# Layer 0's first mixer projections from unsplit fp32 weights, and V's last four blocks kept back

## The chip, the core and the metric

The kernel runs on one core of a Trainium2 chip. The time is device microseconds of one execution. The engines are named as in the profile: PE is TensorE (PEld its weight loads), DVE VectorE, ACT ScalarE, POOL GpSimd, SP SyncE, whose queue issues every DMA of this kernel. The times given are three runs of the kernel and one more execution that the hardware profiler recorded.

## What is computed

Two layers on x (256 tokens by 1024, fp32). A layer modulates a normalised x by vectors that come from a conditioning vector c, projects it into chunks, mixes tokens in three ways (a state-space mixer with a convolution, block-sparse attention, sliding-window attention), adds the result, and then looks up product-key experts.

```python
cond = jax.nn.silu(c)
for l in range(DEPTH):
    mod = cond @ ada_w[l] + ada_b[l]
    sh1, sc1, g1, sh2, sc2, g2 = [m[:, None, :] for m in jnp.split(mod, 6, axis=-1)]
    h = rms_norm(x, norm1_g[l]) * (1.0 + sc1) + sh1
    proj = h @ w_in[l]
    z, xbc, dt_raw, mq, mk, mv, sq, sk, sv = jnp.split(proj, offsets, axis=-1)
    ...
    y = jnp.concatenate([y_ssd, y_moba, y_swa], axis=-1) @ w_out[l]
    x = x + g1 * y
    h = rms_norm(x, norm2_g[l]) * (1.0 + sc2) + sh2
    x = x + g2 * peer_ffn(h, peer_wq[l], peer_k1[l], peer_k2[l], peer_u[l], peer_v[l])
return rms_norm(x, final_g)
```

`peer_ffn` makes queries h @ wq for 8 heads, scores them against two key sets, keeps the top 16, and sums act times V over 16384 experts; here that is computed densely, U first (128 blocks of 128 experts), then V.

## The kernel before, in words

**Split products.** Nearly every product is made from reduced-precision parts: `split` (L151) turns a fetched weight tile into a high part (ScalarE cast, L159, tile `wH`) and a low part (a subtraction, L162, tile `wL`; on VectorE for "v", on GpSimd in two halves for "h"), and `mm3` (L165) does three matmuls, high x high, high x low, low x high. h is split in the same way into `hs` (`hH`, `hL`; L258, L259). Weight tiles come through `fetch` (L145), a ring of five `raw` tiles of 512 KB; `wH` and `wL` are rings of three.

**Layer 0's start.** `cond_row` (L117) loads c as one row, spreads it over 128 partitions with two matmuls against ones (L127) and applies SiLU. A modulation column is one VectorE operation (`ada_use`, L177): a row tile of `ada` (512.5 KB) times the row of c, summed. Layer 0 needs 40 such rows (vectors 0 to 4, eight each); they come through the same `raw` ring as the weights. The first 16 give the shift and scale of h; h is made in four quarters of 256 channels (`norm_banks` L237 transposes x into PSUM, `norm_h` L245 scales it). While the quarters come, the chunks mq, mk and sq are projected in pieces that the table `FIRST` orders (L46). The other 24 rows are handed out two per fetched tile by `later` (L455). After the scores of the MoBA heads the stages run in the order of the string `ORDER` (L47): `rest` is the chunk with the values and dt, c0 to c3 convolve the chunks xbc0 to xbc3, mv, mp, ss, sv, sp are MoBA values and output and the same of the sliding window (with its own chunk sk), seg, tok, stb, cb and st belong to the state-space mixer, z0 and z1 are gates.

**The scheduler.** The program is written in this order, and a scheduler with a model of its own then puts each engine's instructions into a fixed list; each engine runs its list in order.

**Experts.** In `peer` (L671) the queries go head by head (`query`, L713), the split of their weights half on GpSimd. U and V stages follow with TensorE in a steady stream; `steps` (L952) gives, in layer 0's V stage, another c row and 56 modulation rows for layer 1, through `ada_ahead` (L184), which fetches three rows ahead into four tiles. V sums 128 blocks into four PSUM banks (`v_parts`, L888); the last two (`LAST = 2`, L56) are taken bank by bank, so that the first banks are finished earlier. Then the residual is added, the next layer's norm is taken, or at the end the final norm and the output.

```python
            first = {n: [bank(b) for b in kinds] for n, kinds in (("mq", ("pa", "pa")), ("mk", ("pa", "pa")), ("sq", ("pb", "pb")))}
            part = {n: proj_parts(pcs, wl, *off[n], 2) for n, pcs in first.items()}
            for p, names in enumerate(FIRST):
                banks = norm_banks(xn, p, 1, "pc")
                ...
                norm_h(xp, banks, colt, modc, COLS["n1"], 0, 1, p)
                for n in post.split():
                    next(part[n])
```

Of the kernel before, what the change touches and what calls it, by code (L numbers as in the profile page):

```python
# [45 lines left out]
FIRST = (("- - - mq", "mq"), ("mk mk - sq sq", "mq mk sq"), ("mq - mk -", "mq mk"), ("sq sq", "mq mk sq"))  # L46
ORDER = "rest c0 mv c1 mp seg ss c2 z0 sv c3 tok stb z1 cb st sp"  # L47
# [8 lines left out]
LAST = 2  # L56
# [25 lines left out]
def trunk(ctx: ExitStack, tc: tile.TileContext, x_in, c_in, ada, cols, rows, w_in, w_out, wq, keysT, uT, vT, fg, out, dbg=None):  # L82
# [67 lines left out]

    def split(src, low="v", pool=None):  # L151
# [4 lines left out]
        else:  # L156
            h = pool.tile([P, 1024], F32R, tag="oH", name="oH", bufs=2)
            lo = pool.tile([P, 1024], F32R, tag="oL", name="oL", bufs=2)
# [21 lines left out]
    def ada_steps(l, m, modc, pool):  # L180

        return [lambda k=k: ada_use(m, k, fetch(ada[l, m * KD + k]), modc, conds[pool]) for k in range(KD)]

    def ada_ahead(jobs, pool):  # L184

        items = [(l, m, k, modc) for l, m, modc in jobs for k in range(KD)]
# [3 lines left out]
        def load(i):  # L190
            if i < len(items):
                l, m, k = items[i][:3]
                held[i] = pool.tile([P, D + 1], F32, tag="adaw", name="adaw", bufs=AHEAD + 1)
                nc.sync.dma_start(held[i], ada[l, m * KD + k])

        def step(i):
# [5 lines left out]
            ada_use(m, k, held.pop(i), modc, conds[pool])  # L202
# [10 lines left out]
    def norm_rows(pool, xt, c):  # L213

        ss = pool.tile([P, 2], F32, tag="hs", name="hs", bufs=2)
        for n in range(2):
            junk = pool.tile([P, 512], F32, tag="t2k", name="junk", bufs=3)
            A.activation(junk, xt[:, c, n * 512:(n + 1) * 512], AF.Square, scale=1.0 / 32.0, accum_out=ss[:, n:n + 1])  # L218
# [5 lines left out]

    pin = [None]
# [19 lines left out]
    def norm_h(pool, banks, colt, modc, gcol, sh, sc, k20=0):  # L245
# [684 lines left out]
    for l in range(DEPTH):  # L930
        ada0 = {}

        def early(pool, k0, n):
            if l:
                return []
# [118 lines left out]
```

## Time and profile before

| what | value |
|---|---|
| three runs | 1953.8, 1957.2, 1955.97 us; median 1955.97 |
| the profiled execution | 1956.04 us, its span 1954.3 us |
| granted TensorE clock, mean | 0.981 |
| busy: PE, DVE, ACT, POOL | 1875.9, 1430.5, 966.3, 498.1 us |
| share of the span: PE, DVE, ACT, POOL | 96%, 73%, 49%, 25% |
| DMA moved | 376.53 MB, 193 GB/s over the span |
| modulation rows through `raw`, through `adaw` | 40 and 56 issues of 512.5 KB |

The shares are means over stages that differ: most of the span is the U and V stages, where PE is always busy. How the 78 us in which PE is not busy lie in time is read from stretches of the span, and what ends a wait there from the waits and the timeline. A row of the timeline begins with its start and its duration; matmuls overlap, so the cost of one is the distance to the next one's start.

### The profile page before, as it was taken

To read this page: it belongs to the slowest core of one execution; us is meant where nothing else is said; L and a number is where in the kernel's file an instruction comes from. 1 tells how busy PE (TensorE), PEld (TensorE's weight loads), DVE (VectorE), ACT (ScalarE), POOL (GpSimd) and SP (SyncE) were. 2 spreads that over 40 slices of the span, in tenths; PEclk is the share of its full clock that TensorE was granted. 3 is DMA by queue.
4 is the path that set the end of the run, shared out by engine and by line. 5 is a ranking of instruction groups with operands and counts; after the bars stand their busy time and mean duration, and the time that the engine had idled before them with its cause. 6 is when DMAs were issued, how large, how long until landed. Compare 5 with 4: busy or idle time off the path is not lost. (4 is left out here: it accounts for less than half of the span.)

```text
span 1954.3 us, 33671 instructions
## 1 busy us (share of the span) xinstructions
PE 1875.9 (96%) x12864; PEld 1714.5 (88%) x12864; DVE 1430.5 (73%) x2679; ACT 966.3 (49%) x1502; POOL 498.1 (25%) x303
## 2 busy tenths in 40 slices
PE   4898999999999999999989989999999999999998
PEld 3786999999999888888878789999999998888886
DVE  6866799889963898966667669968899346666665
ACT  3464445444444454545547444455444445555544
POOL 5675799100024001000001167960000320000001
PEclk8898999999999999999989989999999999999999
DMA  7863455444455999866543344554444555655553
GB/s 276 288 211 116 162 182 182 167 162 153 161 166 172 380 348 350 312 199 195 192 131 123 118 143 150 186 178 159 160 155 160 173 193 190 223 196 193 193 194 116
DMA packets 103557, 376.53 MB, mean 193 GB/s; under 512 B 12002, under 2 KB 12258, under 8 KB 102756
## 3 DMA queue, kind: packets, MB, share of 16 engines
q1 hardware_dynamic: 103396, 374.39, 56.3%
q8 instruction: 100, 1.64, 0.3%
q14 instruction: 61, 0.50, 0.1%
HBM read 371.20 MB, written 3.15 MB: 192 GB/s over the span
## 5 line engine op out<-in xcount | busy, mean ns | idle before, releaser
L159 ACT CAST wH<-raw 128x1024 fp32r<-128x1024 f32 (+1 forms) x602 | 629.3, 1046 | 530.7 <-PE pu L167 349.9
L162 DVE TENSOR_TENSOR wL<-raw,wH 128x1024 fp32r<-128x1024 f32 x437 | 535.3, 1226 | 223.6 <-ACT wH L159 222.8
L162 POOL TENSOR_TENSOR wL<-raw,wH 128x512 fp32r<-128x512 f32 (+2 forms) x224 | 438.4, 1977 | 595.7 <-ACT wH L159 586.0
L166 PE MATMUL pu<-hH,wH 128*128 128x256 f32 x2048 | 581.2, 284 | 3.9 <-ACT act L693 3.9
L168 PE MATMUL pu<-hH,wL 128*128 128x256 f32 x2048 | 575.7, 281 | 0.0
L167 PE MATMUL pu<-hL,wH 128*128 128x256 f32 x2048 | 575.4, 281 | 0.0
L167 PE MATMUL pacc<-wL,aH 128*128 128x512 f32 x1024 | 399.2, 390 | 0.0
L168 PE MATMUL pacc<-wH,aL 128*128 128x512 f32 x1024 | 398.5, 389 | 0.0
L166 PEld LDWEIGHTS pu<-hH,wH 128*128 128x128 f32 x2048 | 386.9, 189 | 4.6 <-ACT act L693 4.6
L167 PEld LDWEIGHTS pu<-hL,wH 128*128 128x128 f32 x2048 | 387.1, 189 | 0.0
L168 PEld LDWEIGHTS pu<-hH,wL 128*128 128x128 f32 x2048 | 386.5, 189 | 0.0
L166 PE MATMUL pacc<-wH,aH 128*128 128x512 f32 x1024 | 277.4, 389 | 0.0
L892 ACT CAST aH<-act 128x256 fp32r<-128x256 f32 x256 | 104.0, 408 | 340.3 <-PE pacc L167 339.0
L167 PEld LDWEIGHTS pacc<-wL,aH 128*128 128x128 f32 x1024 | 192.2, 188 | 40.4 <-DVE wL L162 0.8
L168 PEld LDWEIGHTS pacc<-wH,aL 128*128 128x128 f32 x1024 | 192.2, 188 | 39.7
L166 PEld LDWEIGHTS pacc<-wH,aH 128*128 128x128 f32 x1024 | 192.1, 188 | 39.8
L893 DVE TENSOR_TENSOR aL<-act,aH 128x256 fp32r<-128x256 f32 x256 | 108.4, 425 | 108.6 <-ACT aH L892 108.2
L980 POOL TENSOR_TENSOR x<-x,fgb 128x512 f32<-128x512 f32 x2 | 3.4, 1700 | 352.4 <-ACT junk L218 352.4
L166 PE MATMUL pa<-hH,wH 128*128 128x256 f32 x256 | 75.7, 308 | 12.5 <-ACT hH L258 8.7
L167 PE MATMUL pa<-hL,wH 128*128 128x256 f32 x256 | 76.4, 301 | 1.9 <-DVE hL L259 1.8
L168 PE MATMUL pa<-hH,wL 128*128 128x256 f32 x256 | 75.6, 299 | 0.9 <-POOL wL L162 0.9
L854 DVE SCALAR_TENSOR_TENSOR act<-pc,act 128x160 f32<-128x160 f32 (+30 forms) x126 | 38.5, 306 | 44.5 <-PE pc L848 44.3
(428 smaller groups left out, 2470.9 us busy)
## 6 DMA issues: line engine op xcount, KB each, us to landing
raw<-in_uT_dram SPq DMA_DIRECT2D x256, 512.0 KB, 3.6
raw<-in_vT_dram SPq DMA_DIRECT2D x256, 512.0 KB, 4.4
adaw<-in_ada_dram SPq DMA_DIRECT2D x56, 512.5 KB, 5.9
raw<-in_ada_dram SPq DMA_DIRECT2D x40, 512.5 KB, 4.9
raw<-in_w_in_dram SPq DMA_DIRECT2D x38, 512.0 KB, 4.8
raw<-in_wq_dram SPq DMA_DIRECT2D x32, 512.0 KB, 3.6
raw<-in_w_out_dram SPq DMA_DIRECT2D x16, 512.0 KB, 3.9
raw<-in_w_in_dram SPq DMA_DIRECT2D x8, 392.0 KB, 3.5
```

The source lines that it names most:

```text
L159: A.copy(h[:, :n], src)
L162: eng.tensor_tensor(out=lo[:, o:o + step], in0=src[:, o:o + step], in1=h[:, o:o + step].bitcast(F32), op=ALU.subtract)
L166: T.matmul(o, l[0], r[0], start=start, stop=False)
L167: T.matmul(o, l[0], r[1], start=False, stop=False)
L168: T.matmul(o, l[1], r[0], start=False, stop=stop)
L854: V.scalar_tensor_tensor(out=a, in0=pv[:, lo:hi, :], scalar=1.0 / WSCALE, in1=a, op0=ALU.mult, op1=ALU.mult)
L892: A.copy(aH, act)
L893: V.tensor_tensor(out=aL, in0=act, in1=aH.bitcast(F32), op=ALU.subtract)
L980: (V if c else G).tensor_tensor(out=xt[:, c, cs], in0=xt[:, c, cs], in1=fgb[:, cs], op=ALU.mult)
```

## The change

Six edits. (1) In layer 0 the chunks mq, mk, sq, xbc0 and xbc1 are projected together, from unsplit fp32 weights and unsplit h; two column blocks share a PSUM bank, which five matmuls with a zero tile clear first. The weights come through `fetch_whole`, every second one into a `wH` or `wL` tile. h is kept in four tiles of `wt`, its split parts `hs` are made after the MoBA scores are issued. `rest` and sk use the unsplit products too; in `ORDER` the two convolutions c0 and c1 come before mv. (2) Layer 0's 40 rows go through `ada_ahead` with four tiles (`oH`, `oL`) of their own. (3) c is loaded into all 128 partitions by one broadcast DMA and SiLU is applied in place; x is loaded in two halves, and the second half's squares are summed by VectorE. (4) In layer 1 mq is unsplit, and the parts of h are split behind its products. (5) In both layers query 0 is unsplit and the parts of h are made after it; query 1's low half is made by VectorE. (6) Of V's last blocks four are taken bank by bank instead of two; two of them get their own tiles `held`, in the place of the row pool, which is closed 14 blocks before the end; a layer's residual and norm are written row half by row half.

```diff
+WHOLE0 = "mq mk sq xbc0 xbc1"
+FIRST = (
+    ((WHOLE0, WHOLE0), ("", WHOLE0), (WHOLE0, WHOLE0), ("", WHOLE0)),
+    (("- - - mq", "mq"), ("mk mk - sq sq", "mq mk sq"), ("mq - mk -", "mq mk"), ("sq sq", "mq mk sq")),
+)
+ORDER = (
+    "rest c0 c1 mv ss mp seg c2 z0 sv c3 tok stb z1 cb st sp",
+    "rest c0 mv c1 mp seg ss c2 z0 sv c3 tok stb z1 cb st sp",
+)
...
-LAST = 2
+LAST = 4
+HELD = 2
+ADA_END = 14
...
-        nc.sync.dma_start(row[0:1, 0:D], c_in)
-        ones = st.tile([1, P], F32, tag="raw", name="ones", bufs=RB)
-        G.memset(ones, 1.0)
-        pcs = []
-        for n in range(2):
-            pc = small_bank()
-            T.matmul(pc, ones, row[0:1, n * 512:(n + 1) * 512], start=True, stop=True)
-            pcs.append(pc)
-        for n, pc in enumerate(pcs):
-            A.activation(row[:, n * 512:(n + 1) * 512], pc, AF.Silu)
+        nc.sync.dma_start(row[:, 0:D], c_in.to_broadcast([P, D]))
+        A.activation(row[:, 0:D], row[:, 0:D], AF.Silu)
...
+    def fetch_whole(src):
+
+        n = src.shape[-1]
+        spare[0] += 1
+        if spare[0] % 2:
+            return fetch(src)
+        tag = "wH" if spare[0] % 4 else "wL"
+        t = st.tile([P, 1024], F32, tag=tag, name="whole", bufs=HB)
+        nc.sync.dma_start(t[:, :n], src)
+        return t[:, :n]
...
+    def proj_parts_whole(pcs, src, off, w, step, hw, zeroed=False):
...
+                        T.matmul(pc[:, :S], raw[:, kk * w + cb * P:kk * w + (cb + 1) * P], hw[k // 2][:, k % 2, :], start=k == 0 and not zeroed, stop=k == KD - 1 and (not zeroed or cb == len(pcs) - 1))
...
+                zero = new([P, 4, P], "segr")
+                V.memset(zero, 0.0)
+                for n in WHOLE0.split():
+                    pc = bank("pb" if n == "sq" else "pa")
+                    T.matmul(pc, zero[:, 0, :], zero, start=True, stop=False)
+                    first[n] = [pc[:, b * S:(b + 1) * S] for b in range(2)]
+                    part[n] = proj_parts_whole(first[n], wl, *off[n], 2, whole, True)
...
             def query(h):
-                with pinned() if h == 0 else nullcontext():
-                    pq = proj_channels(wq[l], h * D * 256, 256, lambda q: "h")
+                if h == 0:
+
+                    pq = [bank() for _ in range(2)]
+                    for _ in proj_parts_whole(pq, wq[l], 0, 256, 4, whole2):
+                        pass
+                    for f in whole2_halves:
+                        f()
+                else:
+                    with pinned() if h == 1 else nullcontext():
+                        pq = proj_channels(wq[l], h * D * 256, 256, lambda q: "v" if h == 1 else "h")
...
-            spread(pend, min(1.0, (n + 1) / (NKEY - 8)), len(todo))
-        last = [v_parts(n, low(n)) for n in range(NKEY - LAST, NKEY)]
+            spread(pend, min(1.0, (n + 1) / (NKEY - ADA_END)), len(todo))
+            if n == NKEY - ADA_END:
+
+                right.close()
+                held = right.enter_context(tc.tile_pool(name=f"held{l}", bufs=1, reuse_waits="tile", side="right"))
+        last = [v_parts(n, low(n), held if n < NKEY - LAST + HELD else None) for n in range(NKEY - LAST, NKEY)]
...
+    own = lambda i: mx.tile([P, D + 1], F32, tag="oL" if i % 2 else "oH", name="adaw", bufs=2)
+    adas = ada_ahead([(0, (0, 1), mod[0])] + [(0, (m,), mod[0]) for m in (2, 3, 4)], own, conds[mx]) if l == 0 else []
```

SyncE's queue at the start of layer 0, first before (behind the loads of the columns, c, x and `rowt`; `in_ada` are the modulation rows, `in_w_in` weight halves):

```order
L148 DMA raw<-in_ada_dram 128x1025 x4
L174 DMA colt<-in_cols_dram 128x112
L148 DMA raw<-in_w_in_dram 128x1024
L148 DMA raw<-in_ada_dram 128x1025
L148 DMA raw<-in_w_in_dram 128x1024
L148 DMA raw<-in_ada_dram 128x1025 x3
```

and now, from the same place (`whole` is a weight half in a `wH` or `wL` tile):

```order
L204 DMA adaw<-in_ada_dram 128x1025 x4
L149 DMA raw<-in_w_in_dram 128x1024
L162 DMA whole<-in_w_in_dram 128x1024
L149 DMA raw<-in_w_in_dram 128x1024
L162 DMA whole<-in_w_in_dram 128x1024
L149 DMA raw<-in_w_in_dram 128x1024
L188 DMA colt<-in_cols_dram 128x112
L204 DMA adaw<-in_ada_dram 128x1025 x8
```

Five weight halves now follow the first four rows at once, and rows and weights no longer share one ring.

VectorE's list around the third xbc chunk, before: `ynam` are the normalised MoBA rows, `conv` with 128x255 the first step of a convolution.

```order
L178 SCALAR_TENSOR_TENSOR raw,modc<-raw,crow 128x1025
L376 TENSOR_SCALAR ynam<-conv,yamr 128x256
L207 TENSOR_SCALAR yamm<-ss 128x1
L178 SCALAR_TENSOR_TENSOR raw,modc<-raw,crow 128x1025
L475 SCALAR_TENSOR_TENSOR conv<-pa,colt,conv 128x255
L475 SCALAR_TENSOR_TENSOR conv<-pa,colt,conv 128x254
L376 TENSOR_SCALAR ynam<-conv,yamr 128x256
```

Now, at the same rows of the MoBA norm:

```order
L443 TENSOR_SCALAR ynam<-conv,yamr 128x256
L217 TENSOR_SCALAR yamm<-ss 128x1
L192 SCALAR_TENSOR_TENSOR adaw,modc<-adaw,crow 128x1025
L443 TENSOR_SCALAR ynam<-conv,yamr 128x256
L192 SCALAR_TENSOR_TENSOR adaw,modc<-adaw,crow 128x1025 x2
L423 SCALAR_TENSOR_TENSOR yL<-pc,colt,yH 128x256
L423 SCALAR_TENSOR_TENSOR yL<-pa,colt,yH 128x256
L192 SCALAR_TENSOR_TENSOR adaw,modc<-adaw,crow 128x1025 x2
```

The convolution of xbc1 has moved ahead of the MoBA norm; 36 of the 40 rows stand before its last `ynam`, where 34 did.

TensorE's list ahead of the third xbc chunk, now (`L420` transposes `ynam`, `L644` is seg, `L180` the first split product of xbc2):

```order
L636 MATMUL pb<-a,mgt 128x8
L637 MATMUL pb<-a,mle 128x8
L420 MATMUL pc<-ident,ynam 128x128
L420 MATMUL pa<-ident,ynam 128x128
L644 MATMUL pa<-segr,mgt 128x512
L420 MATMUL pc<-ident,ynam 128x128
L420 MATMUL pa<-ident,ynam 128x128
L644 MATMUL pc<-segr,mgt 128x512
L180 MATMUL pc<-hH,wH 128x256
```

Before, the same place read:

```order
L353 MATMUL pa<-ident,ynam 128x128
L353 MATMUL pb<-ident,ynam 128x128
L553 MATMUL pb<-segr,mgt 128x512
L406 MATMUL pc<-sk,sq 128x128
L407 MATMUL pc<-sk,sq 128x256
L406 MATMUL pb<-sk,sq 128x128
L407 MATMUL pb<-sk,sq 128x256
L553 MATMUL pa<-segr,mgt 128x512
```

The scores of the sliding window, which stood between the MoBA transposes and xbc2, have moved ahead of the transposes.

## Rows read from the trace of the kernel before

**Rows 1.** Busy time of each engine (instructions), granted clock, DMA share, GB/s, by stretch.

```profile
40.00:60.00 20.00, 13.35 (x86) 12.54 (x87) 17.21 (x26) 7.41 (x14) 11.06 (x7) 0.74 0.82 283
80.00:100.00 20.00, 16.22 (x114) 14.38 (x112) 19.27 (x35) 10.66 (x17) 17.41 (x11) 0.92 0.78 280
650.00:700.00 50.00, 50.00 (x230) 41.57 (x229) 48.62 (x75) 23.58 (x36) 0.00 (x0) 1.00 1.01 389
900.00:950.00 50.00, 50.00 (x223) 41.39 (x222) 30.78 (x37) 24.46 (x36) 0.00 (x0) 1.00 0.60 197
```

The columns are the stretch, its length, then PE, PEld, DVE, ACT, POOL, the clock as a share of full speed, the DMA engines' busy share and GB/s.

**Rows 2.** Waits of SyncE's queue, 0 to 200 us: total, times, longest.

```profile
SPq L148 <- POOL wL L162: 64.5, 28, 4.9
SPq L148 <- DVE raw L178: 49.7, 28, 5.9
```

**Rows 3.** Timeline, 22.5 to 24 us: two modulation rows on VectorE and a GpSimd split.

```profile
22.66 1.23 DVE L178 SCALAR_TENSOR_TENSOR raw<-raw,crow 128x1025 f32<-128x1025 f32 x1
...
23.04 1.98 POOL L162 TENSOR_TENSOR wL<-raw,wH 128x512 fp32r<-128x512 f32 x1 [3.01 <-ACT wH L159]
...
23.80 2.31 DVE L178 SCALAR_TENSOR_TENSOR raw<-raw,crow 128x1025 f32<-128x1025 f32 x1
```

**Rows 4.** Groups by line and shape, VectorE, 0 to 125 us: busy, mean ns, waits.

```profile
L178 DVE SCALAR_TENSOR_TENSOR raw<-raw,crow 128x1025 f32<-128x1025 f32 x40 | 61.1, 1538 | 11.2 <-DMA raw<-in_ada_dram 7.5 <-POOL wL L162 2.0 <-ACT crow L130 1.7
```

**Rows 5.** Timeline of TensorE: starts of matmuls that follow each other.

```profile
58.34 0.59 PE L407 MATMUL pa<-mk,mq 64*128 64x256 f32 x2
58.77 0.27 PE L406 MATMUL pa<-mk,mq 64*128 64x128 f32 x1
...
104.63 1.02 PE L553 MATMUL pb<-segr,mgt 128*128 128x512 f32 x2
105.58 0.49 PE L406 MATMUL pc<-sk,sq 64*128 64x128 f32 x2
...
200.48 0.28 PE L166 MATMUL pc<-hH,wH 128*128 128x256 f32 x1
200.60 0.28 PE L167 MATMUL pc<-hL,wH 128*128 128x256 f32 x1
```

**Rows 6.** Timeline, marks of layer 0: waited h, its last quarter, xbc2's first matmul, the masked product.

```profile
45.29 1.22 PE L166 MATMUL pa<-hH,wH 128*128 128x256 f32 x4 [6.75 <-ACT hH L258]
...
50.83 0.55 DVE L257 TENSOR_SCALAR h<-pc,acol,modc 128x256 f32<-128x256 f32 x1
...
110.46 0.39 PE L166 MATMUL pa<-hH,wH 128*128 128x256 f32 x1
...
145.90 0.69 DVE L587 TENSOR_TENSOR cbm<-pb,mle 128x512 f32<-128x512 f32 x1 [2.29 <-PE pb L585]
```

**Rows 7.** Timeline, layer 0's second norm to the first query's scores.

```profile
179.22 0.89 DVE L234 TENSOR_SCALAR xn<-x,hr 128x512 f32<-128x512 f32 x2 [0.44 <-POOL hr L222]
...
180.89 2.88 DVE L234 TENSOR_SCALAR xn<-x,hr 128x512 f32<-128x512 f32 x2 [0.66 <-POOL hr L222]
...
185.90 0.58 PE L166 MATMUL pa<-hH,wH 128*128 128x256 f32 x1 [0.96 <-ACT hH L258]
...
200.84 1.05 PE L725 MATMUL pa<-kt,q 128*128 128x128 f32 x8
```

**Rows 8.** Timeline of TensorE in layer 0's V stage: the conditioning row.

```profile
645.17 1.12 PE L127 MATMUL pb<-crow,ones 1*128 1x512 f32 x2
...
647.08 0.50 PE L167 MATMUL pacc<-wL,aH 128*128 128x512 f32 x1
```

**Rows 9.** The broadcast load of the last gain, from the view of that tile.

```profile
DMA to landing us min/median/max: 8.5/8.5/8.5
```

**Rows 10.** Timeline of TensorE between the layers.

```profile
990.53 0.39 PE L167 MATMUL pacc<-wL,aH 128*128 128x512 f32 x1
990.76 0.39 PE L168 MATMUL pacc<-wH,aL 128*128 128x512 f32 x1
...
1000.31 0.56 PE L166 MATMUL pa<-hH,wH 128*128 128x256 f32 x1
```

**Rows 11.** Timeline, the end: the last matmul and the last output operation of ScalarE.

```profile
1944.77 0.39 PE L168 MATMUL pacc<-wH,aL 128*128 128x512 f32 x1
...
1950.34 0.72 ACT L986 ACTIVATE o<-x,hr 128x512 f32<-128x512 f32 x1 [1.29 <-POOL hr L222]
```

More of the change, by code (lines that the diff above doesn't have):

```diff
@@ L256, in norm_h, with half @@
                 else:
-                    V.tensor_scalar(out=h32[:, q, :], in0=src, scalar1=acol[:, k:k + 1], scalar2=modc[:, sh, k:k + 1], op0=ALU.mult, op1=ALU.add)
-            A.copy(hs[0][:, 2 * k2:2 * k2 + 2, :], h32)
-            V.tensor_tensor(out=hs[1][:, 2 * k2:2 * k2 + 2, :], in0=h32, in1=hs[0][:, 2 * k2:2 * k2 + 2, :].bitcast(F32), op=ALU.subtract)
+                    d = V.tensor_scalar(out=h32[:, q, :], in0=src, scalar1=acol[:, k:k + 1], scalar2=modc[:, sh, k:k + 1], op0=ALU.mult, op1=ALU.add)
+                    done[0] = d.ins
+                    if whole is not None and len(banks) > 1:
+                        pin[0] = d.ins
+            def half(k2=k2, h32=h32):
+                A.copy(hs[0][:, 2 * k2:2 * k2 + 2, :], h32)
+                V.tensor_tensor(out=hs[1][:, 2 * k2:2 * k2 + 2, :], in0=h32, in1=hs[0][:, 2 * k2:2 * k2 + 2, :].bitcast(F32), op=ALU.subtract)
+            if whole is None:
+                half()
+            else:
+                halves.append(half)
+        return halves
     def gated_add(pool, xt, c, n, acc, gb):
@@ L450, in put @@
                     put_y(self.yn, self.blk0, 2)
-            todo = late(mx)
+            todo = list(late)
             due = [0.0]
@@ L463, in conv @@
             def conv(q):
-                for cb, pc in enumerate(proj_channels(wl, *off[f"xbc{q}"])):
+                for cb, pc in enumerate(first.get(f"xbc{q}") or proj_channels(wl, *off[f"xbc{q}"])):
                     b = 2 * q + cb
@@ L503, in mixers @@
             tick[0] = later
+            if l == 0:
+                proj_tokens_rest = lambda: proj_tokens_whole(wl, *off["rest"], whole)
+            else:
+                proj_tokens_rest = lambda: proj_tokens(wl, *off["rest"])
             mq = to_sb(first["mq"], "mq")
@@ L509, in mixers @@
             moba.scores()
+            if halves:
+                with tc.issue_after(done[0]):
+                    for f in halves:
+                        f()
             vx = new([P, NC, 6, 65], "vx")
@@ L518, in values_dt @@
             def values_dt():
-                for c, pc in enumerate(proj_tokens(wl, *off["rest"])):
+                for c, pc in enumerate(proj_tokens_rest()):
                     V.tensor_tensor(out=dtp[:, c, :], in0=pc[:, 0:8], in1=rowt[:, 0:8], op=ALU.add)
@@ L610, in mixers @@
             }
-            for name in ORDER.split():
+            for name in ORDER[l].split():
                 stages[name]()
@@ L976, in trunk @@
             rs.append(norm_rows(xp, xt, c))
+            if not last:
+                xn.append(norm_scaled(xp, xt, c, rs[c]))
         if last:
@@ L987, in trunk @@
                 nc.sync.dma_start(out[0, c * P:(c + 1) * P, cs], o)
-        else:
-            xn = [norm_scaled(xp, xt, c, rs[c]) for c in range(NC)]
         if dbg:
```

137 lines of the change are left out of this document (94 added, 43 removed).

## The prediction

> **What bounds the kernel now.** I read the busy shares by stretch first. In the middle of the program TensorE has no gap: 50.00 of 50 us between 650 and 700 us and again between 900 and 950, with VectorE and ScalarE at 48.62 and 23.58 and at 30.78 and 24.46 [rows 1]. What an edit saves off TensorE there is nothing, and what it takes from TensorE there counts in full. Layer 0's first mixer is another matter: between 40 and 60 us TensorE is busy for 13.35 of 20 us at a granted clock of 0.74, and VectorE for 17.21; between 80 and 100 VectorE has 19.27 of 20 and GpSimd 17.41, while the DMA engines move only 280 GB/s against 389 at 650 us [rows 1]. The waits of SyncE's queue say why they move so little: in the first 200 us it stood 64.5 us behind low halves that GpSimd was still making and 49.7 us behind modulation rows that VectorE was still using, because both sit in the ring of five `raw` tiles [rows 2]. And the two engines slow each other: the use of one modulation row took 1.23 us at 22.66 and 2.31 us at 23.80, under a split that GpSimd began at 23.04 [rows 3]; over the first 125 us the forty took 61.1 us, 1.538 each [rows 4]. So this stage is held by VectorE, GpSimd and buffers, not by TensorE.
>
> **The price of an unsplit product.** A split product is three matmuls 0.12 us apart, 0.36 us for 256 columns [rows 5]. An unsplit fp32 one is two instructions in the trace. The nearest rows bound it: a score matmul with 256 columns but 64 rows of weights took 0.43 us for its two halves (58.34 to 58.77), and one with 128 rows and 512 columns took 0.95 us (104.63 to 105.58), so 0.475 for half the columns [rows 5]. I take 0.43, between 0.40 (no drain) and 0.475. It costs TensorE 0.07 us more than the split one and frees ScalarE and GpSimd or VectorE of the split.
>
> A rule prices it too. The Trainium skill's page "FP8 and Floating Point Precision", section "TensorE Precision Notes", says that true fp32 goes through the array in four passes, where the split product here has three. By that alone it would be 4 x 0.12 = 0.48 us, an estimate; the rows with 64 and 128 weights stand on either side of it. With it the last burst of the first stage, 20 products, would end 20 x 0.05 = 1 us later, and the forecast would be 1943 instead of 1942.
>
> **Layer 0's first stage.** Before, the last quarter of h was made at 50.83 us and the MoBA scores began at 58 us (the row at 58.34) with mq, mk and sq done [rows 5, 6]. Now xbc0 and xbc1 are done beside them. The last quarter waits, on VectorE, for the 19th modulation row. Until that has landed the queue has to bring 19 x 0.525 MB, ten weight halves of 0.524, x with 1.05 and the broadcast c with 0.52: 16.8 MB from about 3 us on. At 283 GB/s that ends at 62 us, at 389 at 46 [rows 1]. I take 355 GB/s, so 50.5 us: nearer the upper end, since ten weight halves now have ten places (five `raw`, three `wH`, two `wL`) and the modulation rows four of their own, which removes the two waits of [rows 2]. With the last use (1.2 us) and the column scale the last quarter of h is there at about 51.5; its 20 products cost 20 x 0.43 = 8.6 us, and 1 us goes to a slow clock. The scores begin at 61 us, 3 us later than before, but with 32 products more behind them. The five zero matmuls (0.95 us each by the 512-column row, twice that at half clock) run while x is still on its way, so they cost nothing; without that cover they would cost 5 to 10 us.
>
> **From the scores to the third convolution chunk.** Before, xbc2's matmuls began at 110.46, 52.1 us after the scores [rows 5, 6]. They stand behind the transposes of the normalised MoBA rows, which VectorE makes late in its list. Now the list has no convolution matmuls to wait for, but the same VectorE work: 17 modulation rows, all scores, the dt chain, the convolutions of xbc0 and xbc1. Added: four splits of h that were moved here, 4 x 0.7 = 2.8 us. Saved: GpSimd splits only xbc2 and half of z0 in this time (6 half splits of some 2 us, where it was busy for 17.41 of 20 us before [rows 1]), so 17 x (1.538 - 1.23) = 5.2 us of contention on the rows, half as much again on the other operations, 8 in all; and 17/40 of the 9.5 us that VectorE waited for rows and for GpSimd [rows 4], 4 us. 52.1 + 2.8 - 8 - 4 = 43. TensorE's own work there (rest, MoBA values, sk and the scores, of which rest's 16 products of 392 columns and sk's 8 are 2.3 us dearer unsplit) is some 22 us and hides. So xbc2 begins at 61 + 43 = 104, **6 us earlier**. From there on to the masked C*B product at 145.90 [rows 6] the same four split chunks are left and TensorE is nearly full in both kernels; I take 0 for that, and 0 for what follows up to the residual.
>
> **First query, both layers.** Before, x's second half was scaled in 2.88 us, under six half splits by GpSimd, the first product of query 0 stood at 185.90, and scores at 200.84 [rows 7]. Now query 0 is not split and query 1 is split by VectorE, so the scaling should cost 0.89, as the other half did at 179.22 [rows 7], and the first product needs neither the cast nor the low half: some 2.7 us earlier. Against that 16 x 0.07 = 1.1 us at full clock. Net 1.7 in layer 0, 1.5 in layer 1, where the list is the same. The moved splits of h (four casts, four subtractions) lie under query 0's 7 to 9 us.
>
> **Between the layers.** The two `ones` matmuls of the conditioning row go: TensorE stands at them from 645.17 to 647.08 [rows 8], 1.9 us in a full stage. In their place a broadcast DMA; the like one for the last gain landed after 8.5 us [rows 9], so VectorE may wait some 3 us, which its slack and three split buffers hide. After V's last matmul at 990.76 the first product came at 1000.31 [rows 10]. With four blocks kept back, the sums of rows 0 to 127 are finished 24 matmuls before the end, 0.23 us apart [rows 10], so 5.4 us, instead of 12 matmuls, 2.7, and mq starts from h itself: I take 2.5 us off and 1.1 us on for mq unsplit, **1.4**. Keeping back four blocks costs no TensorE time: VectorE and ScalarE have 40% and 50% to spare there [rows 1] and two blocks get their own places.
>
> **The end.** The last matmul starts at 1944.77, the last output operation at 1950.34 [rows 11]. Rows 0 to 127 will be out of the way by then: 0.9 us.
>
> Sum: 6 + 1.7 + 1.5 + 1.9 + 1.4 + 0.9 = 13.4 us. The profiled execution took 1956.04 (its span 1954.3), the median 1955.97, so they are one: 1956.0 - 13.4 = 1942.6, **1942**.
>
> **Rivals.** (a) *TensorE and DMA set the pace, VectorE does not.* If contention was most of VectorE's load and the DMAs run at 389 GB/s, the scores come at 57 and xbc2 after TensorE's 22 us, say at 84: 26 us earlier instead of 6, 1922. For it: 2.31 against 1.23 us [rows 3]. Against it: in-order, VectorE has 36 of 40 rows ahead of the transposes.
> (b) *The DMA rate stays.* If 283 GB/s is what rows of this size get in a mixed queue, h's last quarter comes at 64, scores at 73.5, xbc2 at 117: 6 us later, which eats the other terms: 1955.
> (c) *TensorE becomes the bound, slower.* The first stage now has 80 products in four bursts with waits for h between; before, TensorE waited 6.75 us for h until 45.29 us [rows 6], and the stretch from 40 to 60 us had a granted clock of 0.74, between the levels of 1.2 and 2.4 GHz [rows 1]. If every burst runs at 1.2 GHz, the stage has 80 x 0.86 = 69 us from 17 us on, the scores come at 86 instead of 61, and the sum turns to 1942 + 25 = 1967. It decides from the point where the scores come 13.4 us later than forecast, at 74 us. Against the whole price speaks the 0.92 between 80 and 100 us, where TensorE was busy for 16.22 of 20 us and waited often [rows 1].
> The Trainium skill ("TensorE: Matmul & The Clock Gate", section "HAM oscillation") describes just that: bursts shorter than the wait for data let the array fall back to half rate each time. By that rule (c) would be the outcome, 1967; this trace agrees in part, with 0.74 at 40 to 60 us.
>
> **How the numbers follow.** Forecast 0.58, from 1931 (contention wholly gone) to 1951 (scores 5 us late, another 4 lost in the reordered layer 1). (a) 0.15, (b) 0.14, (c) 0.13. The range takes in the forecast, half of (a) and (b): 1924 to 1956. A measurement of this kernel tells 0.2%, about 4 us, from no change. Faster: the forecast but for 0.02, (a), and 0.03 of (b), 0.74; same: 0.10; slower: (c) and a part of (b), 0.16.
>
> **What would show it.** Right: scores near 61 us, 19 rows used by 51, xbc2's matmuls at 101 to 107, rows' uses near 1.25 us until GpSimd starts on xbc2; no L127-like matmul near 645; TensorE full in the V stage. Wrong: a granted clock of 0.5 to 0.6 through 20 to 60 us, SyncE's queue still behind GpSimd, TensorE idle before V's last four blocks, or VectorE idle between 60 and 100 us (then (a) or a wait that I have not seen).

## The result and the profile after

The changed kernel takes 1940.71 us, the median of 6 runs (1938.82 to 1947.49), where the kernel before takes 1955.33, also the median of 6, on the same chip: a ratio of 0.9935 with a 95% interval of 0.9920 to 0.9951. The forecast was 1942, faster. A second set of runs, beside other kernels, gave 0.9950 (0.9933 to 0.9968). The execution that was profiled took 1945.66 us, with a span of 1943.9; so its own gain against the 1954.3 of before is 10.4 us, where the medians differ by 14.6. This table follows that gain through the program. The forecast column adds up the prediction's terms.

| mark | before | after | gain so far | forecast so far |
|---|---|---|---|---|
| layer 0, last quarter of h | 50.83 | 51.38 | -0.6 | -0.7 |
| MoBA scores | 58.01 | 62.49 | -4.5 | -3 |
| xbc2's first matmul | 110.46 | 103.78 | 6.7 | 6 |
| masked C*B product | 145.90 | 144.30 | 1.6 | 6 |
| layer 0, residual, first piece | 172.89 | 170.28 | 2.6 | 6 |
| first U product | 241.00 | 234.21 | 6.8 | 7.7 |
| first V product | 638.72 | 636.00 | **2.7** | 7.7 |
| last V product | 990.76 | 986.30 | 4.5 | 9.6 |
| layer 1, residual, first piece | 1124.65 | 1121.42 | **3.2** | 11.0 |
| first U product | 1192.81 | 1184.51 | 8.3 | 12.5 |
| first V product | 1595.77 | 1585.64 | 10.1 | 12.5 |
| last V product | 1944.77 | 1934.89 | 9.9 | 12.5 |
| end of the span | 1954.3 | 1943.9 | 10.4 | 13.4 |

Three places stand out. Of the 6.7 us at xbc2 only 2.6 reach the residual. Layer 0's U stage, which the change was not thought to touch, loses 4.1 us. And from V's last product to layer 1's residual 1.2 us are lost, where a gain was forecast.

Stretches of the changed kernel (start and end, length, then busy us and instructions of PE, PEld, DVE, ACT, POOL, granted clock, DMA share, GB/s); the first two answer to [rows 1]:

```profile
40.00:60.00 20.00, 16.12 (x69) 13.66 (x68) 14.84 (x26) 2.48 (x6) 0.00 (x0) 0.91 1.01 391
80.00:100.00 20.00, 12.75 (x65) 9.93 (x63) 17.79 (x41) 9.52 (x21) 5.78 (x5) 0.77 0.83 293
100.00:120.00 20.00, 18.57 (x112) 15.61 (x111) 10.45 (x20) 10.22 (x19) 11.80 (x9) 0.81 0.27 97
230.00:250.00 20.00, 17.92 (x141) 17.73 (x139) 20.00 (x104) 8.72 (x11) 11.49 (x6) 0.91 0.44 144
```

The last two in the kernel before:

```profile
100.00:120.00 20.00, 18.44 (x119) 15.15 (x117) 18.55 (x35) 12.81 (x18) 13.44 (x10) 0.91 0.77 246
230.00:250.00 20.00, 20.00 (x173) 20.00 (x172) 20.00 (x137) 10.60 (x15) 15.22 (x8) 1.00 0.48 165
```

From 40 to 60 us the DMA engines move 391 GB/s where they moved 283, GpSimd does nothing, and TensorE's clock is 0.91 where it was 0.74. From 80 to 120 us the clock is lower than before (0.77 and 0.81 for 0.92 and 0.91), and from 230 to 250 TensorE, which had no gap there, has one of 2.08 us.

SyncE's waits in the first 200 us, against [rows 2], and VectorE's group of modulation rows in the first 125 us, against [rows 4] (busy, mean ns | idle before):

```profile
SPq L149 <- POOL wL L176: 34.8, 14, 4.9
SPq L204 <- DVE adaw L192: 34.2, 22, 5.3
SPq L149 <- ACT wH L173: 22.0, 10, 12.3
...
L192 DVE SCALAR_TENSOR_TENSOR adaw<-adaw,crow 128x1025 f32<-128x1025 f32 x40 | 51.8, 1309 | 14.8 <-DMA adaw<-in_ada_dram 14.6
```

The queue still waits, but 69 us for GpSimd and for rows where it was 114 (against that, 22.0 for ScalarE's `wH` where it was 8.2), and a row costs 1.31 us where it cost 1.54.

Marks of layer 0 on the timeline (start, duration), against [rows 6, 7]:

```profile
51.97 0.70 PE L360 MATMUL pa<-h,whole 128*128 128x256 f32 x2 [3.88 <-DVE h L284]
...
62.49 0.37 PE L473 MATMUL pa<-mk,mq 64*128 64x128 f32 x1
...
98.27 0.48 PE L420 MATMUL pc<-ident,ynam 128*128 128x128 f32 x1 [4.92 <-DVE yamm L217]
...
103.78 0.80 PE L180 MATMUL pc<-hH,wH 128*128 128x256 f32 x1
...
112.32 0.28 PE L180 MATMUL pa<-wH,hH 128*128 128x256 f32 x1
...
144.30 0.69 DVE L678 TENSOR_TENSOR cbm<-pc,mle 128x512 f32<-128x512 f32 x1 [0.58 <-PE pc L676]
...
178.29 0.88 DVE L250 TENSOR_SCALAR xn<-x,hr 128x512 f32<-128x512 f32 x2 [0.66 <-POOL hr L236]
...
180.12 0.63 PE L360 MATMUL pa<-h,raw 128*128 128x256 f32 x1
```

The transposes ahead of xbc2 now follow a wait of 4.92 us. Its products take from 103.78 to 112.32, 8.5 us: up to 107.58 they stand 0.21 us apart or more, and an unsplit `segr` product of 512 columns stands among them. Before they took 5.8 (110.46 to 116.27). The second half of xn is scaled in 0.88 us, as forecast, and query 0 follows its transposes without a gap on TensorE.

The start of layer 0's U stage, ScalarE and TensorE:

```profile
241.11 1.28 ACT L791 ACT_TABLE_LOAD   x1
242.41 0.60 ACT L791 ACTIVATE act<-pu 128x512 f32<-128x512 f32 x1
243.06 0.39 PE L180 MATMUL pu<-hH,wH 128*128 128x256 f32 x1 [2.08 <-ACT act L791]
...
244.24 0.42 PE L180 MATMUL pu<-hH,wH 128*128 128x256 f32 x1
244.45 0.42 PE L181 MATMUL pu<-hL,wH 128*128 128x256 f32 x1
```

The second U product waits until the first Gelu has read its bank, and that one stands behind a table load. From 244.24 to 247.44 the matmuls stand 0.21 us apart, not 0.12: half clock, 15 matmuls and 1.4 us. That the load takes 1.28 us is also what the Trainium skill says ("ScalarE: Activation LUTs", section "What ACT_TABLE_LOAD costs": 1283 ns); the 1380 ns of draining that it adds are not in this trace, where the load starts 0.02 us behind the cast ahead of it and the Gelu 0.02 us behind the load.

V in layer 0, the gap between the layers, and the end, against [rows 8, 10, 11]:

```profile
644.18 1.07 PE L180 MATMUL pacc<-wH,aH 128*128 128x512 f32 x4
645.09 0.39 PE L181 MATMUL pacc<-wL,aH 128*128 128x512 f32 x1
...
986.30 0.40 PE L182 MATMUL pacc<-wH,aL 128*128 128x512 f32 x1
...
992.30 1.11 PE L258 MATMUL pc<-ident,xn 128*128 128x128 f32 x4 [5.16 <-DVE xn L250]
993.62 0.80 PE L360 MATMUL pa<-h,raw 128*128 128x256 f32 x1 [0.21 <-DVE h L284]
...
1934.89 0.39 PE L182 MATMUL pacc<-wH,aL 128*128 128x512 f32 x1
```

No `ones` matmul stands in V any more: 350.30 us from the first to the last product where it was 352.04. From V's last product to layer 1's first one it is 7.3 us where it was 9.55. The end is 9.0 us behind the last product where it was 9.5.

### The profile page after: what moved, and what is told of

Its sections match the earlier page's. It is cut to its first block, busy times and chain, and to the rows that moved or that the text cites. A ratio compares the mean times of both kernels' runs of the same rounds, so it can differ in the third digit from the quotient of the medians.

```text
span 1943.9 us, 33211 instructions
## 1 busy us (share of the span) xinstructions
PE 1879.8 (97%) x12714; PEld 1707.9 (88%) x12714; DVE 1403.6 (72%) x2686; ACT 939.6 (48%) x1473; POOL 420.2 (22%) x255
## 5 line engine op out<-in xcount | busy, mean ns | idle before, releaser
L173 ACT CAST wH<-raw 128x1024 fp32r<-128x1024 f32 x577 | 602.6, 1045 | 517.2 <-PE pu L181 349.1
L176 DVE TENSOR_TENSOR wL<-raw,wH 128x1024 fp32r<-128x1024 f32 (+1 forms) x435 | 532.9, 1226 | 215.7 <-ACT wH L173 214.7
L180 PE MATMUL pu<-hH,wH 128*128 128x256 f32 x2048 | 581.1, 284 | 6.0 <-ACT act L791 6.0
L176 POOL TENSOR_TENSOR wL<-raw,wH 128x1024 fp32r<-128x1024 f32 (+1 forms) x178 | 365.2, 2071 | 641.0 <-ACT wH L173 620.9
L181 PE MATMUL pacc<-wL,aH 128*128 128x512 f32 x1008 | 393.3, 390 | 0.0
L180 PEld LDWEIGHTS pu<-hH,wH 128*128 128x128 f32 x2048 | 386.4, 189 | 6.8 <-ACT act L791 6.8
L182 PE MATMUL pacc<-wH,aL 128*128 128x512 f32 x1008 | 392.4, 389 | 0.0
L180 PE MATMUL pacc<-wH,aH 128*128 128x512 f32 x1008 | 272.5, 389 | 0.0
L180 PEld LDWEIGHTS pacc<-wH,aH 128*128 128x128 f32 x1008 | 189.3, 188 | 39.5
L192 DVE SCALAR_TENSOR_TENSOR adaw<-adaw,crow 128x1025 f32<-128x1025 f32 x96 | 120.5, 1261 | 17.2 <-DMA adaw<-in_ada_dram 17.1
L236 POOL TENSOR_TENSOR hr<-hm,mhalf 128x1 f32<-128x1 f32 x10 | 6.6, 664 | 285.8 <-DVE hm L234 285.8
L946 DVE TENSOR_TENSOR o<-iotax,idx 128x1024 f16<-128x1024 f16 x64 | 47.0, 735 | 17.2 <-ACT idx L915 17.1
## 6 DMA issues: line engine op xcount, KB each, us to landing
whole<-in_w_in_dram SPq DMA_DIRECT2D x5, 512.0 KB, 10.5
```

Source lines behind the costliest of these rows:

```text
L173: A.copy(h[:, :n], src)
L176: eng.tensor_tensor(out=lo[:, o:o + step], in0=src[:, o:o + step], in1=h[:, o:o + step].bitcast(F32), op=ALU.subtract)
L180: T.matmul(o, l[0], r[0], start=start, stop=False)
L181: T.matmul(o, l[0], r[1], start=False, stop=False)
L182: T.matmul(o, l[1], r[0], start=False, stop=stop)
L192: V.scalar_tensor_tensor(out=src, in0=src, scalar=1.0, in1=cond, op0=ALU.mult, op1=ALU.mult, accum_out=modc[:, m, k:k + 1])
```

## Experiments

Each ran beside the kernel before on the same chip; the ratios are to that. The chips differ from run to run, so two experiments are compared by their ratios. "U stage" is from the first U product to V's first.

**Whose wait is at 243 us?** `bank()` and `small_bank()` deal out the PSUM banks by one counter. The conditioning row of the kernel before called `small_bank` twice at the start of the program. The change drops these calls, so from there on layer 0 gets pb where it would have got pc, and the other way round; in layer 1, after two more calls are dropped, the count agrees again. The last query's scores now lie in pb, the pool of the U products. *flip* moves the counter on around the query loop, and changes no instruction and no order, only banks:

```diff
+            turn[0] += 2
             qs = [query(0)]
...
+            turn[0] -= 2
             gelu = [u_pair(ip, act1[:, 2 * ip:2 * ip + 2, :]) for ip in range(1, NA // 2 - LEAD)]
```

> The changed kernel with the counter that deals out the PSUM banks moved on by two ahead of the query loop and back behind it, in both layers, so that the last query's scores lie in pc and not in pb, the pool from which the U products take their banks. Bank theory: layer 0's U stage lost 4.07 us against the kernel before (401.67 from its first product to V's first, where it was 397.61) because the second U product had to wait 2.08 us for the first Gelu to free its bank, and half clock followed. Then both layers' U stages take 397.6 us, no wait for act of 2.08 us is left, and the median falls from 1940.7 by 4.2 to 8, to 1933 to 1937. Rival: the lost time is the clock's own and comes back behind another wait; then the waits only move and the median stays within 1940 to 1942.

Measured: 1931.97 us, 0.9891 (0.9875 to 0.9906), the fastest kernel here, and faster than the 1933 to 1937 that the bank theory gave. Its U stages take 398.76 and 398.08, and neither wait is left (same columns as the stretches above):

```profile
230.00:250.00 20.00, 20.00 (x172) 20.00 (x172) 20.00 (x72) 10.31 (x13) 16.58 (x7) 1.00 0.48 159
```

*before_flip0* does the reverse, in the kernel before and in layer 0 alone:

```diff
+            turn[0] += 2 * (l == 0)
             qs = [query(0)]
...
+            turn[0] -= 2 * (l == 0)
```

> The kernel before with the same move of the bank counter around the query loop, in layer 0 alone, so that the last query's scores now lie in pb. Bank theory: layer 0's U stage grows from 397.61 us by 2.1 to 4.1, to 399.7 to 401.7, with a wait of 2.08 us for act at its start; the median goes from 1955.3 to 1957.4 to 1959.4. Rival (the clock's own, or something else of the change): it stays 1955.3 within 1 us.

Measured: 1.0030 (1.0017 to 1.0043), 1959.51 against 1953.96. The stage grew from 397.72 to 401.77 between the two profiles, 4.1 of the 5.5 us, with the wait in it:

```profile
249.49 0.58 PE L166 MATMUL pu<-hH,wH 128*128 128x256 f32 x1 [2.08 <-ACT act L693]
```

So the wait and its price in the U stage are shown in both directions. Over all profiles here, the 11 U stages with that wait took 400.0 to 403.0 us and the 13 without it 397.7 to 399.8. But this is not all of flip: of its 13.8 us of span against the changed kernel's profile, the U stages carry 6.1. The other 7.7 lie where the instructions and their order are the same in both: 2.7 ahead of layer 0's U stage, and 5.0 between layer 0's last V product and layer 1's first U product, where the clock fell in the changed kernel's profile and, after the first burst, not in flip's. Why flip's four runs (1931.7 to 1932.9) all had the better course stays open.

**What carries the first stage?** *split0* is the changed kernel with layer 0's projections split and in the old order, but with the rows' own tiles.

```diff
-            if l:
+            if True:
                 first = {n: [bank(b) for b in kinds] for n, kinds in (("mq", ("pa", "pa")), ("mk", ("pa", "pa")), ("sq", ("pb", "pb")))}
...
-            for p, names in enumerate(FIRST[l]):
+            for p, names in enumerate(FIRST[1]):
...
-            for name in ORDER[l].split():
+            for name in ORDER[1].split():
...
```

> The changed kernel with layer 0's projections split again and in the order of the kernel before; the modulation rows keep their own four tiles, and the broadcast conditioning row, the unsplit first queries and V's kept blocks stay. Theory of the prediction: most of layer 0's gain is the GpSimd work that goes, so rows take 1.5 us again, xbc2 begins near 110, the U stage some 4 to 6.7 us later than in the changed kernel; 1944 to 1947. Rival (the ring): the SyncE waits behind modulation rows were what held the stage, and their own tiles alone give it; xbc2 at 103 to 106, 1940 to 1942.

Measured: 0.9982 (0.9973 to 0.9991), 1950.40 us, slower than either theory; xbc2 at 112.30, the residual at 176.80, the U stage at 240.66. *ring_f* is the other half alone: unsplit weights, on top of flip, with the rows back in the raw ring. They are still fetched three ahead there, which the kernel before did not do, so they hold more of the ring than they did.

```diff
-        own = lambda i: mx.tile([P, D + 1], F32, tag="oL" if i % 2 else "oH", name="adaw", bufs=2)
+        own = lambda i: st.tile([P, D + 1], F32, tag="raw", name="adaw", bufs=RB)
```

> The kernel of flip (1931.97 us, layer 0's U stage begun at 231.46) with layer 0's modulation rows back in the ring of five raw tiles, all else kept. Theory that the unsplit weights carry the gain of layer 0 (in split0 own tiles alone left xbc2 and the residual no earlier than in the kernel before): the MoBA scores stay within 2 us of 62.6, the U stage begins within 1.5 us of 231.5, and the median is 1931 to 1934. Rival (own tiles and unsplit weights are both needed): SyncE waits behind rows again, last h quarter at 55 or later, scores at 66 or later, U stage at 235 to 239, 1935 to 1940.

Measured: 0.9942 (0.9924 to 0.9960), 1942.05; scores at 63.06, as the first theory had it, but xbc2 at 111.49, the residual at 177.02 and the U stage at 240.89. SyncE's waits and the rows of split0, then of ring_f:

```profile
SPq L149 <- POOL wL L176: 64.5, 26, 4.6
...
L192 DVE SCALAR_TENSOR_TENSOR adaw<-adaw,crow 128x1025 f32<-128x1025 f32 x40 | 60.1, 1516 | 5.9 <-DMA adaw<-in_ada_dram 5.8
```

```profile
SPq L204 <- DVE adaw L192: 40.5, 20, 3.7
SPq L149 <- POOL wL L176: 27.8, 11, 4.9
SPq L149 <- DVE adaw L192: 13.6, 7, 4.5
...
L192 DVE SCALAR_TENSOR_TENSOR adaw<-adaw,crow 128x1025 f32<-128x1025 f32 x40 | 50.5, 1268 | 26.3 <-DMA adaw<-in_ada_dram 24.9 <-issue 1.3
```

With the split, GpSimd holds the queue for 64.5 us as before and rows cost 1.52. With the ring, rows cost 1.27 but VectorE waits 24.9 us for them, 14.6 with own tiles. Either part alone has the residual 4 us later than before (172.89); both together have it 2.6 us earlier, 4.3 in flip. Neither theory of split0's pair holds alone: with one part, the wait moves to what the other part would have freed. How much of ring_f's wait comes from fetching three ahead was not tried.

**Does VectorE's list set xbc2, and what is that worth?** *hold* orders layer 0's last 16 rows behind a norm, with 24 ahead of the last `ynam` instead of 36. The mark moves on with every norm, so ten of the 16 stand behind the last `ynam` and six behind the last `ynas`, the sliding window's, at 127.91 us.

```diff
-                V.tensor_scalar(out=o, in0=src, scalar1=r, scalar2=None, op0=ALU.mult)
+                held_by[0] = V.tensor_scalar(out=o, in0=src, scalar1=r, scalar2=None, op0=ALU.mult).ins
...
-                    todo.pop(0)()
+                    with tc.issue_after(held_by[0]) if l == 0 and held_by[0] else nullcontext():
+                        todo.pop(0)()
```

> The changed kernel with the modulation rows that come after the first 24 of layer 0 ordered behind the last normalised MoBA row ynam on VectorE: 24 rows stand ahead of it, where 36 did. Theory of the prediction (VectorE's list sets the start of xbc2): twelve rows of 1.25 us less, so ynam some 10 to 15 us earlier, xbc2 at 89 to 95 where it was 103.78; TensorE's stretch of 2.75 busy us of 10 from 90 to 100 us goes, and with it the granted clock of 0.62 behind it; VectorE, at 30% from 110 to 130 us, takes the rows there. Median 1931 to 1936. Rival (DMA or TensorE sets it): ynam waits for its values or xbc2 for its weights; xbc2 at 99 to 104, 1939 to 1941. Rival on the other side: the late rows now hold the weights' transfers in SyncE's queue or the gate row; xbc2 early, but the residual later than 170.3 us, 1942 to 1946.

Measured: 0.9951 (0.9937 to 0.9965), no better than the changed kernel. xbc2 began at 93.73 and the output projection at 132.70 (136.89), but the residual at 170.71 (170.28): the second rival. *hold2*, on top of flip, puts nine rows behind `ynam` and seven behind the masked product.

```diff
-                due[0] += RATE
+                due[0] += 1.0 if l == 0 and held_by[0] else RATE
...
-                V.tensor_tensor(out=cbm, in0=pcb.rearrange("p (a b) -> p a b", a=4), in1=mle[:, None, :].to_broadcast([P, 4, P]), op=ALU.mult)
+                held_by[0] = V.tensor_tensor(out=cbm, in0=pcb.rearrange("p (a b) -> p a b", a=4), in1=mle[:, None, :].to_broadcast([P, 4, P]), op=ALU.mult).ins
```

> The kernel of flip with layer 0's modulation rows spread: 24 ahead of the last ynam on VectorE as in hold, nine behind it, and the last seven behind the masked C*B product. In hold xbc2 began 10 us earlier (93.73) and the output projection 4.2 (132.70), but then TensorE waited 6.44 us for yL, which stood behind six rows on VectorE, and the residual came at the old time. Theory (VectorE's list sets this stage at every point, rows ahead of what TensorE waits for are the price): with those rows out of the way, the output projection begins at 131 to 133, cbm by 141, the U stage at 226 to 229 where flip has 231.5; 1926 to 1930. Rival (the sum of VectorE's and TensorE's work, not its order, fills the stage): the wait moves to the residual or to the second norm, which needs the last rows; U stage at 230 to 233, 1931 to 1934.

Measured: 0.9929 (0.9915 to 0.9943), 1938.38, with the masked product at 134.53 (144.02 in flip) and the residual at 168.09 (168.58). That is slower than flip and than both theories: in the profiles 2.5 us of it lie between layer 0's residual and its first U product, and 5.0 between the layers' V and U stages, where the edit changes nothing. From hold the first two rows, from hold2 the last two:

```profile
93.73 0.39 PE L180 MATMUL pc<-hH,wH 128*128 128x256 f32 x1 [0.69 <-ACT wt L648]
141.46 0.79 PE L182 MATMUL pa<-wH,yL 128*128 128x512 f32 x1 [6.44 <-DVE yL L423]
```

```profile
138.49 2.30 DVE L192 SCALAR_TENSOR_TENSOR adaw<-adaw,crow 128x1025 f32<-128x1025 f32 x1
157.48 0.90 PE L429 MATMUL pa<-ident,yns 128*128 128x128 f32 x3 [8.60 <-DVE ysm L217]
```

That VectorE's list sets xbc2 is right: twelve rows fewer, 10 us earlier. That an earlier xbc2 is worth anything is not borne out by these two orders. The rows have to run before the second norm, and in both orders TensorE waits behind them later: 6.44 us for yL, or 8.60 for the last norm, where a row costs 2.30 us beside GpSimd. Ten us won at xbc2 or at the masked product reach the residual as -0.4 and 0.5. Rows between 110 and 120 us, where VectorE was busy for 4.68 of 10 us in hold and 3.45 in hold2, were not tried.

**Query 0.** *q0split_f* is flip with query 0 split again in both layers and query 1's low half back on GpSimd, as before; the 10.8 us below belong to both.

```diff
-            whole2_halves[:] = norm_h(xp, norm_banks(xn), colt, modc, COLS["n2"], 3, 4, 0, whole2)
+            norm_h(xp, norm_banks(xn), colt, modc, COLS["n2"], 3, 4)
...
-                    for f in whole2_halves:
-                        f()
...
-                    with pinned() if h == 1 else nullcontext():
-                        pq = proj_channels(wq[l], h * D * 256, 256, lambda q: "v" if h == 1 else "h")
+                with pinned() if h == 0 else nullcontext():
+                    pq = proj_channels(wq[l], h * D * 256, 256, lambda q: "h")
```

> The kernel of flip with query 0 split again in both layers (low halves half by half on GpSimd, query 1 too, as before). Theory of the traces: from the last residual piece to the first query's scores the kernel before took 27.95 us in layer 0 and the changed one 23.76, so the U stage begins 4 us later in layer 0 and about as much in layer 1, xn's second half costs 2.9 us again and query 0 waits for hH; 1938 to 1941. Theory of the prediction's terms (1.7 and 1.5): 1935 to 1936. Rival (covered anyway): 1932 to 1933.

Measured: 0.9971 (0.9960 to 0.9982), 1946.78, dearer than every theory. From the residual to the first U product it takes 67.98 us in layer 0 and 68.29 in layer 1, where flip takes 62.88 and 62.62: 10.8 us. (Most of the rest of its 17.8 us of span is 5.1 in layer 1's mixer and 1.9 ahead of layer 0's residual, which the edit does not touch.) xn's second half and query 0's first product in it:

```profile
178.47 2.88 DVE L250 TENSOR_SCALAR xn<-x,hr 128x512 f32<-128x512 f32 x2 [0.66 <-POOL hr L236]
...
183.48 0.58 PE L180 MATMUL pa<-hH,wH 128*128 128x256 f32 x1 [0.96 <-ACT hH L290]
```

The 2.88 us of [rows 7] are back, and the wait for the cast.

**V's last blocks.** *last2_f* is flip with two blocks kept back.

```diff
-LAST = 4
-HELD = 2
-ADA_END = 14
+LAST = 2
+HELD = 0
+ADA_END = 8
```

> The kernel of flip with two V blocks kept back in the place of four, without the two blocks' own places, and the rows of the next layer spread as before. Theory of the prediction: 2.5 us between the layers and 0.9 at the end are the kept blocks' work, so 1935 to 1936, with the gap of TensorE between V's last matmul and the next layer's first transposes at 8 us where it is 5.6, and the tail at 9.9 where it is 9.0. Rival (the gap is the norm's own chain behind the last sums, not the first rows'): the traces of before and after show gaps of 5.46 and 5.16 us; the edit is worth 0 to 0.8 us, 1932 to 1933.

Measured: 0.9899 (0.9884 to 0.9913), 1932.81; within the interval of flip. From V's last product to the transposes that wait:

```profile
978.68 0.39 PE L182 MATMUL pacc<-wH,aL 128*128 128x512 f32 x1
...
984.52 0.69 PE L258 MATMUL pc<-ident,xn 128*128 128x128 f32 x2 [5.45 <-DVE xn L250]
```

The gap is 5.84 us; with four blocks it is 6.00 in the changed kernel and in flip. The end is 9.67 us behind the last product, 9.05 in flip. The rival holds: the gap is the norm of the last rows. The kept blocks are still worth something behind it: layer 1's first product comes 7.33 us after V's last one in flip and 8.12 here. Against that V is 0.24 us longer with four blocks, in each layer. In sum some 0.9 us.

**What the clock costs.** *warm* is flip with five idle matmuls in the gap between the layers, whose sum nothing uses.

```diff
-        T.matmul(o, l[1], r[0], start=False, stop=stop)
+        last_mm[0] = T.matmul(o, l[1], r[0], start=False, stop=stop).ins
...
+        if not last:
+            with tc.issue_after(last_mm[0]):
+                pw = ps_b.tile([P, 512], F32, tag="pb", name="pb")
+                for i in range(5):
+                    T.matmul(pw, ident, gb[:, 0:512], start=i == 0, stop=i == 4)
```

> The kernel of flip with five idle fp32 matmuls of 512 columns (some 4.8 us at full clock, their sum is used by nothing) on TensorE behind layer 0's last V matmul, where it waits 5.17 us for xn. Clock theory: the wait is what lowers the granted clock to 0.66 in the 10 us around it; without it layer 1's first burst runs at 0.12 us a split matmul and the U stage of layer 1 begins 2.5 to 3.5 us earlier (from V's last matmul, 193.22 us in flip, to 190 to 191); 1928.5 to 1929.5. Rival (the clock falls for another reason, or the next wait holds the stage anyway): 1931 to 1933, and 1934 or more if the matmuls last into the time when xn is there.

Measured: 0.9900 (0.9886 to 0.9914), 1933.66, no gain over flip. Ten us from V's last product, and the ten from 50 us on, of warm, then of flip:

```profile
981.74:991.74 10.00, 8.69 (x37) 5.49 (x36) 7.12 (x13) 6.88 (x12) 0.55 (x1) 1.00 0.28 82
1031.74:1041.74 10.00, 8.24 (x53) 7.35 (x52) 8.32 (x18) 8.72 (x15) 2.21 (x3) 0.86 0.44 145
```

```profile
980.51:990.51 10.00, 4.62 (x16) 3.41 (x15) 6.67 (x12) 6.85 (x12) 0.56 (x1) 0.68 0.27 82
1030.51:1040.51 10.00, 8.23 (x65) 7.35 (x65) 8.36 (x18) 8.26 (x13) 2.22 (x3) 1.00 0.35 119
```

The first half of the theory holds: without the gap the clock stays at 1.00, and layer 1 is 1.76 us ahead 55 us later. But there, behind the wait of 1.31 us that both kernels have, the clock falls in warm and not in flip, and the gain is gone: the residual comes 132.5 us behind V's last product in warm, 130.6 in flip.

**The changed kernel again**, on hold2's chip.

> The changed kernel itself, on the same chip as hold2, as the reference for what the bank counter is worth: with the medians of flip, last2_f and warm (0.989 to 0.990 of the kernel before) the bank theory has it at 0.9935 of the kernel before, 6 to 9 us above flip, and scattered over 1938 to 1947 as its first runs were, since half-clock stretches follow its two waits of 2.08 us in some executions and not in others. Rival (the difference was the chip's): 0.990 to 0.991.

Measured: 1942.83 (1938.76 to 1946.47), 0.9950 (0.9933 to 0.9968). Its U stages took 400.02 and 401.46, 1.3 and 3.4 us longer than flip's, with the same two waits. So flip's lead over it is not the chip's. But of the 10.9 us between the two spans these are 4.6; the rest lies again ahead of layer 0's U stage (1.6) and between the layers' V and U stages (4.6), in the same instructions.

## Why the prediction was right, and where it was not

The time was right, 1942 against 1940.7 and 1942.8, but partly by chance. In the profile the first stage gave 3.4 us less than forecast, the stretch from V to layer 1's residual 2.6 less, and a loss of 4.1 in layer 0's U stage was not foreseen. Against that the first queries gave 6.0 more, and layer 1's U stage came out 1.8 shorter, where a wait that both kernels have was followed by half clock before and not after.

- **Price of an unsplit product**: right at full clock. In query 0 eight instructions, four products, stand from 183.17 to 184.90, 0.43 us each (the four ahead of them, from 180.12, took 0.76 each, mostly at half clock):

```profile
183.17 1.89 PE L360 MATMUL pc<-h,raw 128*128 128x256 f32 x8
184.90 1.46 PE L360 MATMUL pa<-h,raw 128*128 128x256 f32 x6
```

  The four passes that the Trainium skill names ("FP8 and Floating Point Precision", section "TensorE Precision Notes") would be 0.108 us each here. The prediction's estimate of 4 x 0.12 = 0.48 is 10% more than this trace shows. Its two rows, 0.43 and 0.475, both lie below 0.48, not on either side of it, and its lower bound of 0.40 stands in no row.
- **Layer 0's first stage**: right in each step up to xbc2. The last quarter of h came at 51.4 (51.5), the scores at 62.5 (61; the clock halved behind a wait of 3.88 us, and the last burst took 10.5 us, not 9.6), xbc2 at 103.8 (104). That it takes both the weights and the rows' own tiles, as the prediction had it, is shown by split0 and ring_f, for rows that are fetched three ahead.
- **"From there on ... I take 0"**: the step that failed. Of 6.7 us 2.6 reached the residual. Xbc2 ran 2.7 us longer, at half clock behind the wait for `ynam` and with the `segr` product in it. At the output projection the lead was 4.7 us (136.89 for 141.54). From there to the residual TensorE waits 4.8 us (0.78 for `ynas`, 1.69 for `wt`, 2.33 for the last norm) where it waited 3.2, so it was not as full as the prediction had it. hold and hold2 show that a start moved by 10 us gives nothing as long as VectorE's rows stand ahead of a later step; whether they have a free place was not settled.
- **First query**: right in its mechanism, too small. 1.7 and 1.5 us were forecast; from the residual to the first U product the traces gain 4.2 (63.93 for 68.11) and 5.1 (63.09 for 68.16), and q0split_f lost 5.1 and 5.7. What was left out is the clock. Between 180 and 200 us it was 0.74 before and is 0.93 now, where query 0's products no longer wait behind the scaling and the cast (the kernel before, then the changed one):

```profile
180.00:200.00 20.00, 16.90 (x106) 15.28 (x104) 9.12 (x12) 8.38 (x14) 15.07 (x12) 0.74 0.44 150
```

```profile
180.00:200.00 20.00, 20.00 (x134) 18.77 (x133) 10.01 (x37) 9.27 (x17) 8.61 (x7) 0.93 0.55 176
```

- **The `ones` matmuls**: 1.74 us for 1.9. But their removal was priced by the instructions alone. It also dropped two turns of the bank counter, and that cost 4.1 us at the U stage: flip and before_flip0.
- **Between the layers**: 1.4 us were forecast up to layer 1's residual; the changed kernel's profile loses 1.2. Its first product did come 2.2 us earlier behind V's last one, but the kept blocks are 0.8 of that (last2_f), not 2.5. The residual came 135.12 us behind V's last product, where it was 133.89. The ten us behind a wait in layer 1's mixer (1.31 us, 1.39 before), and the residual's first piece, of the kernel before, then of the changed one:

```profile
1050.76:1060.76 10.00, 8.97 (x53) 6.02 (x53) 6.82 (x14) 9.36 (x13) 3.72 (x3) 1.00 0.31 105
...
1124.65 0.69 DVE L265 TENSOR_TENSOR xg<-pb,gb 128x512 f32<-128x512 f32 x1 [2.67 <-PE pb L168]
```

```profile
1046.30:1056.30 10.00, 9.13 (x43) 6.04 (x42) 5.72 (x12) 8.05 (x11) 3.46 (x3) 0.83 0.31 99
...
1121.42 0.69 DVE L302 TENSOR_TENSOR xg<-pb,gb 128x512 f32<-128x512 f32 x1 [2.71 <-PE pb L182]
```

  The clock there was 1.00 before and is 0.83 in the changed kernel. flip, with the same instructions, kept 1.00 there and took 130.59 us; the kernel before took 131.85 in before_flip0. So no run shows a size for this term; the clock moves it by more than it is worth.
- **The end**: 0.5 of 0.9.
- **The rivals**: (a) fell, since VectorE has the MoBA rows ready only at 98 us; (b) fell, with 391 GB/s from 40 to 60 us; (c) fell at its place, since the clock was 0.91 there and the scores came at 62.5, not 86. The half rate behind a wait for data that the Trainium skill describes ("TensorE: Matmul & The Clock Gate", section "HAM oscillation") is in the changed kernel's trace in part: behind the waits that end at 51.97, 98.27, 243.06 and 992.30 us, but not behind the one of 2.08 us at 1193.37.

## What to carry to other kernels

An edit that drops or adds an allocation can turn every later one of a rotating pool. Follow the counter to the next place where two rings meet, above all where an engine loads a table. A gain that is traced to one mark is only a gain if the next mark has moved as well: work that must be done before the residual can move the wait instead of ending it. Two parts of a change can each cost their stage time alone and win together, when each frees the resource on which the other would wait.

## What the runs showed of the hardware

A wait of 1.3 or 2.1 us on TensorE is followed by a stretch at half clock in some executions and not in others, at the same place of the same list. The wait of 2.08 us at layer 0's second U product was followed by 15 matmuls at 0.21 us in the changed kernel's first profile, and by none in its second (after_again):

```profile
241.94 0.38 PE L180 MATMUL pu<-hH,wH 128*128 128x256 f32 x1 [2.08 <-ACT act L791]
...
243.10 0.28 PE L180 MATMUL pu<-hH,wH 128*128 128x256 f32 x1
243.22 0.28 PE L181 MATMUL pu<-hL,wH 128*128 128x256 f32 x1
```

The wait of 1.31 us in layer 1's mixer was followed by a clock of 0.83 over ten us in the changed kernel and of 1.00 in flip, whose instructions are the same but for banks. The changed kernel's twelve runs lie between 1938.8 and 1947.5 us, 8.7 us apart, where flip's four lie 1.2 and last2_f's four 3.0 apart. Keeping TensorE busy through one gap (warm) moved the fall to another. What decides it was not settled.
